# The first attention's values in DRAM: one block per attention unit in place of one row per token

## The chip, the cores and the metric

The kernel runs on one core of a Trainium2 chip. The metric is the device time of one execution in microseconds (us); of several runs the median counts. The core has a matrix engine (TensorE, in the profile PE, its weight loads PEld), a vector engine (DVE), a scalar engine (ACT), a general engine (POOL) and a queue for transfers (SyncE, SP). Transfers between on-chip memory (SBUF) and DRAM run on 16 DMA engines, which all queues share.

## What is computed

Two transformer layers over 1024 latent tokens and 256 context tokens, 1280 in all, 1024 wide. Only the first layer's attention matters here:

```python
p_x, p_c = u_x @ ev_w_in[j], u_c @ ev_w_in[j]
aq, ak, av, bq, bk, bv = split_cols(p, EVEN_SPLITS)      # 6 x 512 columns
# A: 4 differential heads, values 128 wide
a = softmax(q1 k1) - lam * softmax(q2 k2);  o = a @ av
# B: 8 neighbourhood heads, values 64 wide: a query at (row, col) of the 16 x 64 grid reads
# a window of 8 rows x 16 columns of latent keys and all 256 context keys
p = softmax(concat([q k_win * scale + bias, q k_ctx * scale]));  o = p_win @ v_win + p_ctx @ v_ctx
```

## The kernel before, in words

The first layer's projections and its attention are two stages that pass queries, keys and values through DRAM.

**Projection** (`qkv_body`). First come 16 query and key blocks, each of which is stored as 128 rows of 1280 tokens (`sq`, `sk`). Then a loop over z = 0 to 3 and over ten token tiles t computes the values, 256 columns at a time. With z below 2 these are the values of A: the 128 x 256 product is copied out of PSUM into a tile `vf` (tag `qf`, two buffers, ACT and DVE in turn, L481) and stored into `sv` (L482). With z of 2 or 3 they are the values of B, split into a high and a low part: a tile `vs` of 128 x 512 (tags `qh` and `whl` in turn, two buffers each), which is stored into `svb` (L487). The last seven of these stores go out on POOL's queue, all others on SP's.

**Attention** (`attn0`). There are eight units. Units 0 to 3 are the heads of A: a unit loads its queries and keys (12 transfers) and its values, 128 columns of `sv` (`vd`, L1131). Units 4 to 7 are pairs of heads of B: a unit's 256 columns of `svb` are loaded once for the context (`vc`, L1012) and, for each of four column windows j, as four blocks of 4 grid rows x 32 columns (`vs`, L1018), 16 such loads a unit. Each unit of B also needs six bias tables (`tab`, two transfers each, from `rexp`), to which POOL adds a mask (L1030) before DVE uses them.

**What sets the order.** On PE, DVE, ACT and POOL a table of step offsets (`PATTERN`) orders the steps of the jobs; the program's own order rules the transfers of SP. SP takes one transfer after the other: while one waits (for a buffer, for an earlier transfer, for the data to be stored), all behind it wait. A unit's queries and keys are issued during the unit before; `na_hooks` puts the value and table loads of B at fixed jobs. So SP's order at the turn of two units of B is: 12 query and key loads, four `vs`, a store of an output (`so`), four `vs`, two `tab`, `vc`, four `tab`, four `vs`, and so on. POOL also runs in order: a mask whose table has not landed holds up the two memsets (L952, L953) that the next job's transposes on PE need.

Of the kernel before, what the change touches and what calls it, by code (L numbers as in the profile page):

```python
# [10 lines left out]
F32 = mybir.dt.float32  # L11
F32R = mybir.dt.float32r
# [7 lines left out]
P = 128  # L20
# [4 lines left out]
T = NX + NC_  # L25
# [3 lines left out]
HD = 64  # L29
# [51 lines left out]
class Kernel:  # L81
# [211 lines left out]
    def qkv_body(self, es):  # L293
        nc, io = self.nc, self.io
        sb, ps = self.pool(es, "qkv"), self.pool(es, "qkvp", bufs=8, space=PSUM)
        u = [(self.t(sb, [P, KT, 640], f"uh{g}", F32R), self.t(sb, [P, KT, 640], f"ul{g}", F32R)) for g in range(2)]
        w_in = io["ev_w_in"][0].rearrange("(k p) n -> p k n", p=P)
        self.sq = [self.t(self.dram, [2, P, T], f"sq{i}", F32R) for i in range(NU)]
        self.sk = [self.t(self.dram, [2, P, T], f"sk{i}", F32R) for i in range(NU)]
        self.sv = self.t(self.dram, [T, 512], "sv")  # L300
        self.svb = self.t(self.dram, [T, 8, 2, HD], "svb", F32R)
        bg = [(0, ch, hf, 2) for ch in (2, 3, 4, 5) for hf in range(2)]
        bg += [(1, ch, hf, 2) for ch in (0, 1) for hf in range(2)]
        vw = {}
# [6 lines left out]
        def load_w(n):  # L311
            if n < len(cols):
                wf[n] = self.t(sb, [P, KT, P], "wf", bufs=3)
                self.dma(wf[n], w_in[:, :, cols[n]:cols[n] + P])

        def split_v(n):
            z, q = (n - NQ) // 2, (n - NQ) % 2
            if q == 0:
                vw[z] = self.t(vpool, [P, 2, KT, 256], "vw", F32R, bufs=2)
            sl = slice(q * P, q * P + P)  # L320
            self.split(vw[z][:, 0, :, sl], vw[z][:, 1, :, sl], wf[n])

        with ExitStack() as e2:
# [56 lines left out]
            with ExitStack() as e3:  # L380
                st = self.pool(e3, "start")
                h, pt, m = {}, {}, self.modcol[0]
# [59 lines left out]
            def gen_steps(k):  # L442
                accs.extend(a for a in (next(gen) for _ in range(k)) if a)

            def fin():
                for _ in range(len(accs)):
                    self.mod_fin(ps, accs.pop(0))
# [17 lines left out]
            for z in range(4):  # L465
                for t in range(NT):
                    if t in (1, 3):
                        load_w(NQ + 2 * z + (t + 1) // 2 + 2)
                    if t == 0:
                        gen_steps(5)  # L470
                    if t == 8:
                        fin()
                    if t in (4, 6) and z < 3:
                        split_v(NQ + 2 * z + t // 2)
                    g, c0 = t // 5, (t % 5) * P
                    pp = self.t(ps, [P, 256], "ps")
                    self.mm3(pp, lambda k: (u[g][0][:, k, c0:c0 + P], u[g][1][:, k, c0:c0 + P]),
                             lambda k: (vw[z][:, 0, k, :], vw[z][:, 1, k, :]), KT)
                    if z < 2:
                        vf = self.t(qk, [P, 256], "qf", bufs=2)  # L480
                        (nc.scalar.copy if t % 2 else nc.vector.tensor_copy)(vf, pp)  # L481
                        self.dma(self.sv[t * P:(t + 1) * P, z * 256:(z + 1) * 256], vf)  # L482
                    else:
                        vs = self.t(qk, [P, 4, 2, HD], ("qh", "whl")[t % 2], F32R, bufs=2)
                        self.split(vs[:, :, 0, :], vs[:, :, 1, :], pp.rearrange("p (h d) -> p h d", d=HD))

                        (nc.gpsimd if z == 3 and t > 2 else nc.sync).dma_start(  # L487
                            out=self.svb[t * P:(t + 1) * P, (z - 2) * 4:(z - 1) * 4].bitcast(F32), in_=vs.bitcast(F32))


    def rsqrt_exp(self, sb, v, shape, eps):
# [514 lines left out]

    def na_values(self, sb, u, j):

        src = self.svb[:, (u - 4) * 2:(u - 3) * 2].rearrange("t h a d -> t (h a d)")
        if j < 0:  # L1010
            v = self.vs[u, "c"] = self.t(sb, [P, 2, 2, P], "vc", F32R, bufs=2)
            self.dma(v.rearrange("p t h d -> p t (h d)"), src[NX:T, :].rearrange("(t p) c -> p t c", p=P))  # L1012
        else:
            c0 = (0, 8, 24, 32)[j]
            v = self.vs[u, j] = self.t(sb, [P, 4, 2, P], "vs", F32R, bufs=7)
            for rb in range(4):
                sr = src[rb * 256 + c0:rb * 256 + c0 + 1, :]
                self.dma(v[:, rb].rearrange("p h d -> p (h d)"),  # L1018
                         bass.AP(sr.tensor, sr.offset, [[64 * 1024, 4], [1024, 32], [1, 256]]))

    def na_table(self, sb, u, hh, v):

# [95 lines left out]
    def attn_unit(self, sb, ps, u):  # L1118


        qs, ks, ql = (self.t(sb, [P, 2, T], f"{tag}{u % 2}", F32R) for tag in ("qs", "ks", "ql"))
        for m in range(2):
            rows = slice(m * HD, (m + 1) * HD)
            for half in range(2):
                dst = slice(half * HD, (half + 1) * HD)
                self.dma(ks[dst, m, :], self.sk[u][half, rows, :])
                self.dma(qs[dst, m, :], self.sq[u][0, rows, :])
                self.dma(ql[dst, m, :], self.sq[u][1, rows, :])
        if u < 4:
            v = self.t(sb, [P, NT, P], "vd", bufs=2)  # L1130
            self.dma(v, self.sv[:, u * P:(u + 1) * P].rearrange("(t p) c -> p t c", p=P))  # L1131
        unit = (qs, ks, ql)
        if u < 4:
            return self.diff_jobs(sb, ps, u, unit, v)
        return self.na_jobs(sb, ps, u, unit)
# [1640 lines left out]
```

## Time and profile before

| | us |
|---|---|
| median of 3 runs | 3331.13 (3330.67 to 3339.73) |
| the profiled execution | 3333.32 |
| its span, first to last instruction | 3331.5 |
| TensorE busy | 3054.3 (92% of the span) |
| VectorE busy | 2433.3 (73%) |
| DMA, all queues | 444.68 MB in 369192 packets, 133 GB/s over the span |

The span is cut by time into stages: projection of queries and keys to about 330 us, values of A and B to 425 us, the turn to the attention to 450 us, units 0 to 3 to about 680 us, units 4 to 7 to about 890 us. All that the change touches lies in these 560 us; behind them are the output projection, the feed-forward layers and the second layer. A transfer moves its data in packets, here one for each contiguous piece; a packet of under 512 bytes in these views is the end mark of a transfer. "Share of 16 engines" is the packets' time summed over the engines and divided by 16 times the stretch; it can pass 100% where packets on one engine overlap.

### The profile page before, as it was taken

The page shows a single profiled execution, that of the slowest core. Times are in us where ns is not written, and L with a number is a line of the kernel's source. Part 1 is how long each engine was busy: PE and PEld are TensorE (multiplying, and loading weights), DVE is VectorE, ACT ScalarE, POOL GpSimd, SP SyncE. Part 2 cuts the span into 40 slices and gives each one's busy share as a digit, 9 for nine tenths or more (in the row PEclk, how much of TensorE's full clock was granted, in tenths as well). Part 3 has the DMA queues.
Part 4 walks back from the last instruction along what each step waited for, and adds up shares of the span by engine and source line. Part 5 has one row for each costly group of instructions (what it writes and reads, how often), then busy time and mean ns, then how long its engine had stood idle before and what let it go on. Part 6 is the DMA issues. An engine that isn't in the chain of part 4 may idle for free. (4 is left out here: it accounts for less than half of the span.)

```text
span 3331.5 us, 47831 instructions
## 1 busy us (share of the span) xinstructions
PE 3054.3 (92%) x17519; PEld 2711.9 (81%) x17519; DVE 2433.3 (73%) x4109; ACT 1547.1 (46%) x3186; POOL 1003.3 (30%) x780
## 2 busy tenths in 40 slices
PE   7999989975888899889999999989999799999997
PEld 5999878874777899679999788769997688888875
DVE  5776668875788998588997654448887866665576
ACT  5344357774634444333544336237774432333443
POOL 1345445663453221131331002134543301111021
PEclk9999989997998999999999999989999899999998
DMA  7565564375524333644343444274314322225542
GB/s 228 157 216 190 174 173 104 96 172 153 168 76 139 108 112 98 177 144 124 107 145 89 146 151 170 93 230 103 95 39 146 110 74 83 85 80 179 182 135 89
DMA packets 369192, 444.68 MB, mean 133 GB/s; under 512 B 52430, under 2 KB 265071, under 8 KB 365499
## 3 DMA queue, kind: packets, MB, share of 16 engines
q1 hardware_dynamic: 367629, 438.44, 43.5%
q8 instruction: 138, 2.26, 0.3%
q0 software_dynamic: 848, 3.02, 0.3%
q14 instruction: 97, 0.79, 0.1%
q10 hardware_dynamic: 480, 0.16, 0.0%
HBM read 344.51 MB, written 98.18 MB: 133 GB/s over the span
## 5 line engine op out<-in xcount | busy, mean ns | idle before, releaser
L125 PE MATMUL pc<-u,blk 128*128 128x320 f32 (+1 forms) x3540 | 633.0, 336 | 24.7 <-DVE st L1809 7.0
L125 PEld LDWEIGHTS pc<-u,blk 128*128 128x128 f32 x3540 | 573.0, 192 | 66.0 <-DVE blk L1711 7.8
L125 PE MATMUL pa<-blk,blk 128*128 128x512 f32 x1188 | 292.5, 397 | 19.8 <-DVE blk L1711 17.3
L1708 ACT CAST blk<-big 128x512 fp32r<-128x512 f32 x292 | 178.2, 621 | 263.6 <-DVE big L1804 105.0
L1711 DVE TENSOR_TENSOR blk<-wf,blk 128x512 fp32r<-128x512 f32 x377 | 289.2, 769 | 4.5 <-ACT blk L1708 4.5
L125 PEld LDWEIGHTS pa<-blk,blk 128*128 128x128 f32 x1188 | 226.3, 192 | 74.3 <-issue 10.4
L1708 ACT CAST blk<-wf 128x512 fp32r<-128x512 f32 x377 | 232.3, 619 | 111.6 <-PE pc L125 59.6
L1711 DVE TENSOR_TENSOR blk<-big,blk 128x512 fp32r<-128x512 f32 x292 | 212.0, 726 | 57.5 <-ACT blk L1708 57.4
L125 PE MATMUL pa<-u,blk 128*128 128x320 f32 (+1 forms) x1356 | 241.5, 328 | 9.2 <-DVE pt L1809 8.3
L125 PE MATMUL ps<-uh,whl 128*128 128x320 f32 (+2 forms) x1024 | 234.2, 316 | 8.2 <-DVE whl L122 4.8
L125 PEld LDWEIGHTS pa<-u,blk 128*128 128x128 f32 x1356 | 215.5, 190 | 20.6 <-DVE pt L1809 9.0
L125 PE MATMUL pc<-blk,blk 128*128 128x512 f32 x924 | 220.5, 394 | 5.4 <-DVE blk L1711 5.4
L125 PE MATMUL pa<-big,ohl 128*128 128x512 f32 x756 | 201.8, 404 | 19.0 <-POOL ohl L122 4.9
L125 PEld LDWEIGHTS pc<-blk,blk 128*128 128x128 f32 x924 | 175.1, 190 | 42.8 <-ACT u L113 5.8
L247 POOL TENSOR_TENSOR macc<-mw,macc 128x512 f32<-128x512 f32 x96 | 149.3, 1557 | 172.9 <-ACT mw L244 92.6
L820 POOL TENSOR_SCALAR p<-p,rec 128x384 f32<-128x384 f32 (+1 forms) x160 | 143.0, 909 | 177.0 <-DVE rec L635 153.1
L125 PEld LDWEIGHTS pa<-big,ohl 128*128 128x128 f32 x756 | 146.0, 195 | 52.9 <-POOL ohl L122 9.7
L125 PEld LDWEIGHTS ps<-uh,whl 128*128 128x128 f32 x1024 | 176.8, 193 | 11.6 <-DVE whl L122 6.4
L603 ACT ACTIVATE p<-xps,nm 128x1024 f32<-128x1024 f32 x128 | 143.3, 1119 | 80.8 <-DVE nm L599 74.0
L1286 POOL TENSOR_TENSOR r<-r,rowg 128x1024 f32<-128x1024 f32 x32 | 84.0, 2624 | 315.7 <-ACT r L1277 147.2
L624 DVE TENSOR_REDUCE mx<-xps 128x1 f32<-128x1024 f32 x128 | 156.0, 1219 | 18.7 <-PE xps L125 17.8
L125 PE MATMUL ps<-ul,whl 128*128 128x320 f32 (+2 forms) x512 | 161.4, 315 | 1.8 <-DVE ul L415 1.7
(411 smaller groups left out, 6943.9 us busy)
## 6 DMA issues: line engine op xcount, KB each, us to landing
wf<-in_ffn_w_in SPq DMA_DIRECT2D x132, 512.0 KB
wf<-in_ffn_w_out SPq DMA_DIRECT2D x88, 512.0 KB
mw<-in_mod_w SPq DMA_DIRECT2D x64, 512.0 KB
wf<-in_mod_w SPq DMA_DIRECT2D x32, 512.0 KB
uhl<-sun SPq DMA_DIRECT2D x13, 1024.0 KB
wf<-in_ev_w_in SPq DMA_DIRECT2D x24, 512.0 KB
hid<-r SPq DMA_DIRECT2D x22, 512.0 KB
ks<-sk SPq DMA_DIRECT2D x32, 320.0 KB
```

The costliest lines, as they stand in the source:

```text
L125: self.nc.tensor.matmul(out, lhsT, rhs, start=start, stop=stop)
L247: nc.gpsimd.tensor_tensor(out=acc[n][:, conds - 1, :], in0=w, in1=acc[n][:, conds - 1, :], op=ALU.add)
L603: self.nc.scalar.activation(out=out, in_=in_, func=AF.Exp, scale=scale, bias=st["nm"][:, s:s + 1], accum_out=st["sums"][:, s, part:part + 1])
L624: nc.vector.tensor_reduce(out=st["mx"][:, s, 0:1], in_=st["x", s], axis=AX.X, op=ALU.max)
L820: self.nc.gpsimd.tensor_scalar(out=ap, in0=ap, scalar1=rec, scalar2=0.0, op0=ALU.mult, op1=ALU.add)
L1286: self.nc.gpsimd.tensor_tensor(out=e["r"], in0=e["r"], in1=e["rows"]["g"], op=ALU.mult)
L1708: nc.scalar.copy(hi, src)
L1711: nc.vector.tensor_tensor(out=lo, in0=src, in1=hi, op=ALU.subtract)
```

## The change

The two scratch tensors in DRAM get another layout. `sv` was [1280 tokens, 512 columns], so that a token's row held all four units; it becomes [4 units, 1280 tokens, 128 columns]. `svb` was [1280 tokens, 8 heads, 2 parts, 64], and becomes [4 units, 1280 tokens, 256 columns]. A store writes the columns of two units: before one contiguous piece a token (1 KB in `sv`, 2 KB in `svb`), now two pieces of half the size, in two blocks. A load reads the columns of one unit: pieces of the same size as before (512 bytes from `sv`, 1 KB from `svb`), which now lie next to each other in DRAM where they lay 2 KB and 4 KB apart. 112 transfers have another pattern: 20 stores into `sv`, 20 into `svb`, 4 loads of `vd`, 4 of `vc` and 64 of `vs`. On every engine and queue the instructions stand in the same order as before, and each waits for the same things.

```diff
-        self.sv = self.t(self.dram, [T, 512], "sv")
-        self.svb = self.t(self.dram, [T, 8, 2, HD], "svb", F32R)
+        self.sv = self.t(self.dram, [4, T, P], "sv")
+        self.svb = self.t(self.dram, [4, T, 4 * HD], "svb", F32R)
...
-                        self.dma(self.sv[t * P:(t + 1) * P, z * 256:(z + 1) * 256], vf)
+                        self.dma(self.sv[2 * z:2 * z + 2, t * P:(t + 1) * P, :].rearrange("u t c -> t u c"),
+                                 vf.rearrange("p (u c) -> p u c", u=2))
...
-                            out=self.svb[t * P:(t + 1) * P, (z - 2) * 4:(z - 1) * 4].bitcast(F32), in_=vs.bitcast(F32))
+                            out=self.svb[2 * z - 4:2 * z - 2, t * P:(t + 1) * P, :].rearrange("u t c -> t u c").bitcast(F32),
+                            in_=vs.rearrange("p (u h) a d -> p u (h a d)", u=2).bitcast(F32))
...
-        src = self.svb[:, (u - 4) * 2:(u - 3) * 2].rearrange("t h a d -> t (h a d)")
+        src = self.svb[u - 4]
...
-                         bass.AP(sr.tensor, sr.offset, [[64 * 1024, 4], [1024, 32], [1, 256]]))
+                         bass.AP(sr.tensor, sr.offset, [[64 * 256, 4], [256, 32], [1, 256]]))
...
-            self.dma(v, self.sv[:, u * P:(u + 1) * P].rearrange("(t p) c -> p t c", p=P))
+            self.dma(v, self.sv[u].rearrange("(t p) c -> p t c", p=P))
```

## Rows read from the trace of the kernel before

**Rows 1.** Stretches by stage: busy us of each engine, granted clock, DMA share, GB/s.

```profile
core 0: us, PE busy (x) PEld busy (x) DVE busy (x) ACT busy (x) POOL busy (x), PEclk, DMA share, GB/s
330.00:363.00 33.00, 28.11 (x210) 23.32 (x209) 20.50 (x21) 10.89 (x19) 17.92 (x14) 0.95 0.53 154
395.00:425.00 30.00, 29.84 (x255) 29.64 (x255) 21.41 (x25) 12.18 (x22) 18.54 (x13) 1.00 0.54 177
425.00:450.00 25.00, 18.38 (x132) 17.81 (x131) 4.82 (x11) 2.24 (x6) 5.33 (x8) 0.83 1.04 304
450.00:680.00 230.00, 212.16 (x1503) 190.37 (x1502) 202.34 (x403) 172.62 (x437) 128.02 (x65) 0.97 0.49 114
680.00:890.00 210.00, 145.06 (x1074) 136.87 (x1072) 142.52 (x384) 138.53 (x370) 109.73 (x189) 0.87 0.57 158
```

**Rows 2.** Waits, 325 to 442 us: who waited for whom, us, times, longest.

```profile
ACT qf L481 <- DMA sv<-qf: 29.4, 8, 8.3
...
DVE qf L481 <- DMA sv<-qf: 14.2, 3, 7.0
...
PE ps L125 <- DVE qf L481: 4.7, 2, 4.0
```

**Rows 3.** Transfers of 346.3 to 346.85 us: one store into `sv`, alone.

```profile
DMA packets 145, 0.13 MB, mean 242 GB/s; under 512 B 16, under 2 KB 144, under 8 KB 145
...
q1 hardware_dynamic: 145, 0.13, 72.3%
```

**Rows 4.** Transfers of 66 to 67 us: loads in pieces of 512 bytes.

```profile
DMA packets 674, 0.35 MB, mean 354 GB/s; under 512 B 3, under 2 KB 671, under 8 KB 674
...
q1 hardware_dynamic: 674, 0.35, 117.9%
```

**Rows 5.** Transfers of 1999.9 to 2000.4 us: one store in 512-byte pieces.

```profile
DMA packets 48, 0.02 MB, mean 33 GB/s; under 512 B 16, under 2 KB 48, under 8 KB 48
...
q10 hardware_dynamic: 48, 0.02, 15.5%
```

**Rows 6.** Issues on SP and POOL of the tile `sv`, ns min/median/max.

```profile
L109 SPq DMA_DIRECT2D sv<-qf x20: 319/326/882, 330.9 to 380.4; - x20
L109 SPq DMA_DIRECT2D vd<-sv x4: 366/374/377, 440.2 to 568.7; - x4
```

**Rows 7.** Waits, 426 to 470 us.

```profile
POOL p L732 <- ACT p L603: 16.1, 1, 16.1
...
PE b L125 <- DMA ql<-sq: 6.6, 1, 6.6
```

**Rows 8.** Transfers of 408 to 410 us: stores into `svb`, then a weight load.

```profile
DMA packets 379, 0.71 MB, mean 355 GB/s; under 512 B 32, under 2 KB 32, under 8 KB 379
...
q1 hardware_dynamic: 379, 0.71, 95.7%
```

**Rows 9.** Transfers of 397.5 to 398.4 us: one store into `svb`.

```profile
DMA packets 80, 0.16 MB, mean 182 GB/s; under 512 B 0, under 2 KB 0, under 8 KB 80
...
q1 hardware_dynamic: 80, 0.16, 68.2%
```

**Rows 10.** Waits, 680 to 890 us.

```profile
PE xps L830 <- POOL p L953: 45.0, 3, 20.0
POOL tab L1030 <- DMA tab<-rexp: 42.3, 3, 21.7
...
POOL tab L1030 <- DMA vs<-svb: 8.7, 1, 8.7
```

**Rows 11.** SP's instructions in order of time, 743 to 768 us: start us, us.

```profile
743.76 5.76 SPq L109 DMA_DIRECT2D vs<-svb  x4
749.62 3.93 SPq L1002 DMA_DIRECT2D so<-o  x1
753.59 5.14 SPq L109 DMA_DIRECT2D vs<-svb  x4
758.83 2.66 SPq L109 DMA_DIRECT2D tab<-rexp  x2
761.65 0.47 SPq L109 DMA_DIRECT2D vc<-svb  x1
762.22 4.28 SPq L109 DMA_DIRECT2D tab<-rexp  x4
```

**Rows 12.** Transfers of 638 to 639.5 us: loads of `vs` alone.

```profile
DMA packets 143, 0.14 MB, mean 94 GB/s; under 512 B 5, under 2 KB 143, under 8 KB 143
...
q1 hardware_dynamic: 143, 0.14, 27.1%
```

**Rows 13.** Transfers of 46 to 48 us: loads of `h`, rows of 4 KB side by side.

```profile
DMA packets 205, 0.76 MB, mean 379 GB/s; under 512 B 20, under 2 KB 20, under 8 KB 205
...
q1 hardware_dynamic: 205, 0.76, 95.4%
```

**Rows 14.** Issues of the tile `vs` on SP, ns min/median/max.

```profile
L109 SPq DMA_DIRECT2D vs<-svb x64: 515/1290/3665, 623.8 to 858.0; - x64
```

## The prediction

> **What bounds the kernel now.** I read four views in this order: the stretches by stage, the waits of each stage, SP's instructions at the places where a wait ends on a transfer, and the packets of single transfers. By stage [rows 1], TensorE is nearly full while the values of B are computed (29.84 of 30 us) and works 212.16 of 230 us in units 0 to 3, so transfers can hardly cost anything there. It has gaps in three stretches: 33 - 28.11 = 4.9 us in the values of A, 25 - 18.38 = 6.6 us at the turn to the attention, and 210 - 145.06 = 65 us in units 4 to 7. In each gap the wait that ends last ends on a transfer that the change touches, or on one queued behind such a transfer.
>
> In the values of A, ACT waits 29.4 us in 8 places and DVE 14.2 us in 3 until an earlier store into `sv` has given its tile back; TensorE itself waits 4.7 us for it [rows 2]. At the turn, TensorE waits 6.6 us for the first unit's queries [rows 7], while the DMA engines are full (share 1.04). In units 4 to 7 POOL waits 42.3 us for tables, and 8.7 us in a wait that ends with a load of `vs`; TensorE waits 45.0 us in 3 places for the memsets that POOL does behind them [rows 10]. SP shows why the tables are late: from 743.76 us it issues eight `vs` (5.76 + 5.14 us) with a store between them, and only then the tables [rows 11]. So eight `vs` loads stand on the path at each of three turns.
>
> **The change part by part.** No instruction moves and no wait is added or removed. What can change is what a transfer costs its queue, and how long its packets take.
>
> Stores into `sv`. One store alone took 72.3% of 16 engines for 0.55 us, which is 6.36 us of one engine [rows 3], and 6.36 / 128 = 49.7 ns for a piece of 1 KB. The change makes 256 pieces of 512 bytes out of 128 of 1 KB. No store into `sv` of that kind is in the trace; the nearest rows are loads in 512-byte pieces, 1.179 x 16 us / 674 = 28.0 ns each [rows 4], and a small store, 0.155 x 16 x 0.5 / 48 = 26 ns over all its packets, or 1.24 / 32 = 39 ns if its 16 end marks cost nothing [rows 5]. With 28 ns a store takes 256 x 28 - 128 x 49.7 = 0.81 us more engine time, 0.05 us over 16 engines; with 39 ns, 0.23 us. Below, a piece cannot cost less than half of 49.7 ns unless the price per piece vanishes, so the other end is 0. All 11 waits of ACT and DVE end on such a store: 11 x 0.05 = **0.6 us** (0 to 2.5). I take 28 ns because those pieces ran on full engines. The issue grows too: 0.326 us for one piece a partition, 0.374 for ten [rows 6], at most 0.05 us each, and only the three stores just before the first unit's loads have SP's path behind them: 0.1 us.
>
> By the Trainium skill, "DMA: Bandwidth & Descriptors", section "Why small descriptors are slow (HBM only)", a packet costs about three bus cycles beside its 32-byte beats; an estimate from that page is 38 cycles for two pieces of 512 bytes against 35 for one of 1 KB, 9% more, where the rows above say 13%. The trace is thus on the same side as the rule, and the first term would be 0.4 us instead of 0.6 by the rule.
>
> Stores into `svb`. A 2 KB piece took 0.957 x 16 x 2 / (379 - 32) = 88 ns on full engines [rows 8] and 0.682 x 16 x 0.9 / 80 = 123 ns in a stretch with pauses [rows 9]. Two pieces of 1 KB are 2 x 49.7 = 99 ns: 11 ns more or 24 ns less. An engine takes 8 rows of a store, so one store costs +0.09 or -0.19 us. During z = 2 and 3 TensorE is full and hides it. The last ten stores, three on SP and seven on POOL, run while the first unit's loads fill the DMA engines, and there they add to what TensorE waits for: 10 x 0.09 = **0.9 us** (-1.9 to 0.9). I take the dear end because the engines are full there too. POOL itself has room: after its stores it stands idle for 16.1 us [rows 7].
>
> Loads of `vd` and `vc`. Same pieces, same count; `vd` is needed many us after its issue, in units where TensorE is 92% busy. 0.
>
> Loads of `vs`. Here the layout could pay: 32 pieces of 1 KB lay 4 KB apart and now form one run of 32 KB. While only `vs` was moving, 27.1% of 16 engines were busy, 4.3 engines, at 94 GB/s [rows 12]: each load runs on as many engines as it has blocks of rows, four, and those four were full. A piece took 0.271 x 16 x 1.5 / 143 = 45.5 ns, no more than the 49.7 ns of the 1 KB stores [rows 3], which shows no penalty for the gaps that a dense layout could remove. Rows of 4 KB that do lie side by side took 0.954 x 16 x 2 / 185 = 165 ns, 41.2 ns a KB [rows 13]. So the best that contiguity can give is 45.5 - 41.2 = 4.3 ns a piece, 32 pieces an engine, 8 loads and three turns: 4.3 x 32 x 8 x 3 = 3.3 us; if instead a piece cost the dearest 1 KB price of the trace, 49.7 ns, it would be 3.2 us more. I take **0**: the count of pieces, their size and the four blocks are the same. The cost of issuing, 0.515 us at the least and 1.29 us in the middle [rows 14], is set by the four full engines and stays.
>
> Sum: 0.6 + 0.1 + 0.9 + 0 = +1.6 us. On the profiled execution's own 3333.32 us that is 3334.9; this execution lies 2.2 us above the median of the runs shown, so the median comes to 3331.1 + 1.6 = **3332.7 us**. The unknown terms give -5.2 (0 - 1.9 - 3.3) to +6.7 us (2.5 + 0.1 + 0.9 + 3.2), that is 3326 to 3338.
>
> **The rivals.** *The four engines become sixteen.* If the queue saw the run of 32 KB as one thing and spread a `vs` load over all engines, its issue would fall from about 1.3 us to the 0.515 us that it takes when nothing stands in the way [rows 14]. Eight loads at three turns: 0.78 x 8 x 3 = 18.7 us less, 3313 us. For it: those loads stand on the path at every turn [rows 10, 11], and behind them TensorE is plainly idle. Against it: the pattern still begins with four blocks, which are not next to each other, and [rows 12] fit a rule that counts blocks. The Trainium skill, same page, section "Why a DMA increments its semaphore by 16 and not by 1", says just that: the number of engines is the largest up to 16 that divides the slowest dimension of both sides. By that rule it stays at four; the 4.3 engines of the trace agree. 5%.
>
> *Stores pay by the piece.* If a piece of half the size cost what the whole one did, a store into `sv` would take 6.36 / 16 = 0.40 us longer, and one into `svb` 8 x 88 = 0.70 to 8 x 123 = 0.98 us longer. The place is the values of A with their two tiles (11 x 0.40 = 4.4 us) and the turn to the attention (10 x 0.84 = 8.4 us, the middle): 12.8 us, 3344 us, slower. It decides by itself once a half piece costs over about nine tenths of a whole one, where the sum passes 10 us. For it: these stretches do wait on stores and on full engines [rows 1, 2, 7]. Against it: packets grow with their bytes everywhere in the trace, 28 ns at 512 bytes, 49.7 at 1 KB, 88 at 2 KB, 165 at 4 KB [rows 3, 4, 8, 13]. 5%.
>
> *POOL's stores fall behind.* Seven stores go out on POOL's queue beside the first unit's loads. If twice as many pieces a row slow that queue, the loads get past it, and at most TensorE's wait of 6.6 us shrinks [rows 7]; half of it is 3.3 us, 3328 us. Nothing waits for these stores before units 6 and 7, some 300 us on. 8%.
>
> **How the numbers follow.** The forecast, a change of a few us either way from the terms above, has 82%. About 0.3% (10 us) is what a measurement of this kernel can tell from no change; the forecast and the rival on POOL's queue lie within it, save for a few per cent that the stalls in units 4 to 7 react more than term by term, since the granted clock averaged 0.87 of full speed there [rows 1] and a gap that grows or shrinks takes slow time with it. So the same 88%, faster 7%, slower 5%. The range is the bounds of the terms, 3326 to 3338, and 2 us on either side for the spread of the runs, which went up to 3339.73: 3324 to 3340.
>
> **What would show it.** Right: some 4,000 to 5,000 more packets, the stretch with `vs` alone still at about 4.3 engines and 94 GB/s, eight `vs` still 11 us at each turn, POOL's waits for tables within 3 us of 42.3, and a store into `sv` alone at 7 us of engine time. Wrong: `vs` issues near 0.5 us each with a DMA share near 1, or a store into `sv` at 12 us of engine time and TensorE's gap before 340 us wider by some 4 us.

## The result: 0.6% slower, lost in one place at the turn to the attention

The changed kernel takes 3355.52 us (median of 4 runs, 3353.57 to 3357.48) against 3334.68 us (4 runs) for the kernel before: a ratio of 1.0062, 95% interval 1.0047 to 1.0077. The forecast was 3332.7 us, with a range of 3324 to 3340; the measured time lies 15.5 us above its end. The profiled execution spans 3351.8 us where that of before spanned 3331.5 us. Line numbers are one to three higher in the changed kernel (L481 is now L482, L487 is L489, L603 is L606, L732 is L735, L953 is L956).

The stretches by stage of the changed kernel, with the columns of [rows 1], show where the time stands:

```profile
core 0: us, PE busy (x) PEld busy (x) DVE busy (x) ACT busy (x) POOL busy (x), PEclk, DMA share, GB/s
395.00:425.00 30.00, 30.00 (x258) 30.00 (x258) 20.90 (x23) 11.43 (x22) 17.98 (x12) 1.00 0.56 171
425.00:450.00 25.00, 19.03 (x135) 18.02 (x133) 2.27 (x7) 1.86 (x5) 3.60 (x4) 0.81 1.05 266
450.00:490.00 40.00, 17.41 (x83) 13.70 (x82) 18.68 (x34) 14.39 (x35) 8.98 (x7) 0.65 0.63 157
490.00:690.00 200.00, 186.76 (x1357) 168.53 (x1355) 178.13 (x349) 149.80 (x378) 115.76 (x50) 0.99 0.39 94
690.00:910.00 220.00, 154.66 (x1140) 145.60 (x1138) 150.97 (x409) 147.72 (x397) 116.46 (x201) 0.87 0.60 161
```

Up to 425 us nothing is late: the first load of the attention's keys goes out at 425.28 us, before the change at 425.26. From 450 to 490 us TensorE works 17.41 us and its granted clock falls to 0.65; in the same 40 us of the kernel before it worked 35.61 us at 0.89:

```profile
450.00:490.00 40.00, 35.61 (x217) 30.70 (x216) 34.20 (x66) 29.57 (x74) 15.90 (x6) 0.89 0.60 133
```

After that the work runs as before, only later: the first `vs` load goes out at 644.0 us, before at 623.8 [rows 14], and the last at 877.7 instead of 858.0. So about 20 us are lost in one place and carried to the end.

The waits of the changed kernel from 425 to 480 us (who waited for whom, us in total, times, longest) show the chain:

```profile
POOL svb L489 <- issue: 35.2, 5, 9.0
...
PE xps L125 <- ACT p L606: 21.7, 2, 16.1
...
ACT p L606 <- DMA svb<-qh: 17.5, 1, 17.5
ACT whl L113 <- DMA svb<-whl: 14.2, 3, 9.2
...
ACT qh L113 <- DMA svb<-qh: 11.9, 3, 9.4
```

It is read from the end. TensorE waits 21.7 us for ACT's `p`, the exponentials of the first unit. ACT waits 17.5 us before one `p` until a store of `svb` from a tile `qh` has landed: `p` of the attention stands where the projection's tiles stood. Those stores are the last seven, on POOL's queue, and POOL stands 35.2 us at five of them in idle time called "issue", that is, with no other engine and no landing named as the cause. In order of time, POOL's instructions there (start us, us, idle before):

```profile
426.10 1.02 POOL L489 DMA_DIRECT2D svb<-whl  x1
432.96 0.75 POOL L489 DMA_DIRECT2D svb<-qh  x1 [5.83 <-issue]
442.69 0.73 POOL L489 DMA_DIRECT2D svb<-whl  x1 [8.98 <-issue]
452.26 0.73 POOL L489 DMA_DIRECT2D svb<-qh  x1 [8.84 <-issue]
462.87 0.73 POOL L489 DMA_DIRECT2D svb<-whl  x1 [9.88 <-DVE rho L724]
472.58 0.73 POOL L489 DMA_DIRECT2D svb<-qh  x1 [8.98 <-issue]
475.88 0.73 POOL L489 DMA_DIRECT2D svb<-whl  x1 [2.57 <-issue]
```

From the second to the sixth, a store goes out every 9.6 to 10.6 us, and a store took 9.3 us in the middle from issue to landing. One pause, that before 462.87, is put down to a step of DVE (`rho`), but it is as long as the others. When the stores landed can be seen from ACT, which waits for landings to write into the same tiles:

```profile
442.48 0.37 ACT L113 CAST qh<-ps 128x256 fp32r<-128x256 f32 x1 [9.37 <-DMA svb<-qh]
452.05 0.37 ACT L113 CAST whl<-ps 128x256 fp32r<-128x256 f32 x1 [9.20 <-DMA svb<-whl]
...
475.68 1.11 ACT L606 ACTIVATE p<-xps,nm 128x1024 f32<-128x1024 f32 x1 [17.52 <-DMA svb<-qh]
```

In each of these places POOL's next store follows 0.2 us later, at 442.69, 452.26 and 475.88 us: it goes out when the one before it has landed. In the kernel before, the same seven looked like this:

```profile
426.21 0.87 POOL L487 DMA_DIRECT2D svb<-whl  x1
427.14 0.55 POOL L487 DMA_DIRECT2D svb<-qh  x1
427.83 0.54 POOL L487 DMA_DIRECT2D svb<-whl  x1
433.03 0.55 POOL L487 DMA_DIRECT2D svb<-qh  x1 [4.66 <-issue]
...
441.71 0.54 POOL L487 DMA_DIRECT2D svb<-whl  x1 [2.54 <-DVE whl L122]
```

Three went out without a stop. The fourth left at 433.03 us, 0.2 us after ACT's cast at 432.82, which had waited for the landing of the first. The last of the seven left at 441.71 us, now at 475.88. ACT's `p` then starts at 475.68 us, and TensorE's next matmul at 476.94, after its 16.1 us.

**The theory** (called the ring theory in the expectations): POOL writes an entry for every piece of its transfers into a part of SBUF, the ring, whose size the kernel sets, by `dynamic_dma_scratch_size=512` (bytes a partition) in the function `kernel`. An entry's place is free again when the transfer has landed. With 128 pieces a store three stores fit in at a time, with 256 pieces only one, and POOL stands at the next issue until there is room. Its rivals: that twice as many pieces cost the DMA engines that time, or that the layout of `sv`, or both layouts together, does.

### The profile page after: what moved, and what is told of

It reads as the page before. It is cut to its first block, busy times and chain, and to the rows that moved or that the text cites. A ratio compares the mean times of both kernels' runs of the same rounds, so it can differ in the third digit from the quotient of the medians.

```text
span 3351.8 us, 47831 instructions
## 1 busy us (share of the span) xinstructions
PE 3057.2 (91%) x17519; PEld 2715.5 (81%) x17519; DVE 2434.0 (73%) x4109; ACT 1547.9 (46%) x3186; POOL 1001.8 (30%) x780
## 2 busy tenths in 40 slices
DMA packets 373416, 444.68 MB, mean 133 GB/s; under 512 B 52430, under 2 KB 270959, under 8 KB 369723
## 4 chain that ended last, share of the span: by engine, by line
PE 42%; DVE 9%; DMA 3%; issue 2%; ACT 1%; SPq 1%; POOL 1%; ACTq 0%; DVEq 0%; POOLq 0%
PE pc L125 18%; PE pa L125 17%; PE xps L125 2%; DVE blk L1714 2%; PE ops L125 2%; PE b L833 2%; DVE rs_y L1166 1%; DVE big L1807 1%; PE b L125 1%; SPq L109 1%; DVE r L1262 1%; DVE big L2219 1%; DVE r L1256 0%; DMA eh<-hm 0%; ACT eu L1324 0%
## 5 line engine op out<-in xcount | busy, mean ns | idle before, releaser
L606 ACT ACTIVATE p<-xps,nm 128x1024 f32<-128x1024 f32 x128 | 143.4, 1120 | 92.1 <-DVE nm L602 68.7
```

Source lines behind the costliest of these rows:

```text
L606: self.nc.scalar.activation(out=out, in_=in_, func=AF.Exp, scale=scale, bias=st["nm"][:, s:s + 1], accum_out=st["sums"][:, s, part:part + 1])
```

## The experiments

All ratios are to runs of the kernel before on the same chip; the times in one column come from several chips. The table gives, for each kernel, the store sizes on POOL's queue, what the trace shows of POOL, of TensorE's longest wait from 425 to 485 us, and when the first `vs` went out.

| kernel | ring, bytes | pieces a store | issues before the first stop | POOL's idle time at "issue", us | TensorE's longest wait | first `vs`, us | time, us | ratio (95%) |
|---|---|---|---|---|---|---|---|---|
| before | 512 | 128 | 3 | 4.7 | 6.6, `ql` | 623.8 | 3334.68 | 1 |
| after | 512 | 256 | 1 | 35.2 | 16.1, `p` | 644.0 | 3355.52 | 1.0062 (1.0047 to 1.0077) |
| e3 before | 256 | 128 | 1 | 35.8 | 16.4, `p` | 640.0 | 3352.31 | 1.0057 (1.0044 to 1.0070) |
| e5 `svb` only | 512 | 256 | 1 | 35.2 | 16.0, `p` | 639.1 | 3354.25 | 1.0056 (1.0042 to 1.0069) |
| e4 `sv` only | 512 | 128 | 3 | 4.8 | 3.7 | 622.4 | 3334.61 | 1.0004 (0.9995 to 1.0013) |
| e6 after, halves | 512 | 2 x 128 | 3 halves | 24.2 | 6.5, `ql` | 623.8 | 3336.99 | 1.0009 (0.9999 to 1.0018) |
| e2 after | 768 | 256 | 2 | 14.8 | 6.6, `ql` | 622.1 | 3334.54 | 1.0001 (0.9992 to 1.0010) |
| e1 after | 832 | 256 | 3 | 6.9 | 4.3 | 622.0 | 3339.11 | 1.0021 (1.0011 to 1.0031) |
| e10 before | 768 | 128 | 4 or more | 0 | 5.5, `ql` | 620.7 | 3334.61 | 1.0004 (0.9995 to 1.0013) |
| e9 before | 832 | 128 | 4 or more | 0.2 | 3.9 | 619.9 | 3341.14 | 1.0024 (1.0014 to 1.0034) |
| e11 before, other end moved | 768 | 128 | 4 or more | 0.2 | 5.9, `ql` | 621.5 | 3339.38 | 1.0017 (1.0008 to 1.0026) |
| e12 before, `big` and its end moved | 768 | 128 | 4 or more | 0 | 6.5, `ql` | 620.8 | 3340.18 | 1.0019 (1.0010 to 1.0029) |
| e7 after, ACT's queue | - | 256 | - | - | 10.8, `ql` | 628.9 | 3338.99 | 1.0010 (1.0000 to 1.0019) |
| e8 before, ACT's queue | - | 128 | - | - | 13.3, `ql` | 632.2 | 3342.20 | 1.0018 (1.0010 to 1.0027) |

### The ring alone, made larger under the change and smaller under the kernel before

```
-    nc = bacc.Bacc("TRN2", ..., dynamic_dma_scratch_size=512)
+    nc = bacc.Bacc("TRN2", ..., dynamic_dma_scratch_size=768)   # e1: 832; e3, on the kernel before: 256
```

> The changed kernel with 768 bytes for POOL's ring: room for 576 pieces at the least and under 768 by what the two traces show. R expects two stores in flight and never three: pairs of issues some 8 us apart, the seventh at about 450 to 460 us, and 3337 to 3345 us, no faster than the run with 832 bytes. P and S expect 3355 us as with 512 bytes.

> The changed kernel with 832 instead of 512 bytes a partition for POOL's ring of transfer descriptors; nothing else differs. Theory R (the ring is full): before, three stores of 128 pieces were issued back to back (426.21, 427.14, 427.83 us) and the fourth only at 433.03, after the first had landed; after the change each store of 256 pieces waits for the one before (426.10, 432.96, 442.69, ...). So 512 bytes hold three stores of 128 pieces but not two of 256. With 832 bytes there is room for 1.6 times as much, 624 pieces at the least: two stores of 256, perhaps three. R expects the seven stores issued by about 445 to 455 us instead of 476, and 3335 to 3340 us. Theory P (a piece costs POOL's queue more time, whatever the room): the stores keep their pace of about 9.6 us each, 3355 us. Theory S (the layout of DRAM or the stores into sv cost the time): 3355 us.

> The kernel before, old layout, with the ring cut from 512 to 256 bytes: room for one store of 128 pieces, not for two. R expects the old layout to become slow in the same way: each of POOL's stores waits for the one before, the seventh is issued near 470 us, ACT and TensorE wait for it at the start of the first unit, and the time is 3350 to 3357 us. P and S expect no change, 3335 us, since neither the pieces nor the layout differ from before.

POOL's stores with 768 bytes under the change:

```profile
425.54 1.02 POOL L489 DMA_DIRECT2D svb<-whl  x1
426.61 0.74 POOL L489 DMA_DIRECT2D svb<-qh  x1
432.27 0.73 POOL L489 DMA_DIRECT2D svb<-whl  x1 [4.92 <-issue]
435.65 0.72 POOL L489 DMA_DIRECT2D svb<-qh  x1 [2.64 <-issue]
441.53 0.72 POOL L489 DMA_DIRECT2D svb<-whl  x1 [5.15 <-issue]
```

Two are in flight, and the whole loss is gone (1.0001) with the same layouts, pieces and bytes. That is better than expected: 3334.54 us lies below 3337 to 3345. With 256 bytes the kernel before, with none of the change in it, loses what the change lost, and its trace has the same signature, one store at a time:

```profile
423.81 0.87 POOL L487 DMA_DIRECT2D svb<-whl  x1
430.82 0.56 POOL L487 DMA_DIRECT2D svb<-qh  x1 [6.14 <-issue]
440.15 0.54 POOL L487 DMA_DIRECT2D svb<-whl  x1 [8.77 <-issue]
449.38 0.54 POOL L487 DMA_DIRECT2D svb<-qh  x1 [8.69 <-issue]
```

and, among its waits from 425 to 485 us:

```profile
PE xps L125 <- ACT p L603: 23.1, 3, 16.4
...
ACT p L603 <- DMA svb<-qh: 17.4, 1, 17.4
```

So the ring is shown both ways, the loss taken away and made. The theory that the pieces themselves cost the time falls: e2 moves all of them. With the stop gone, nothing of the change is left that can be measured (0.9992 to 1.0010). With 832 bytes three stores of 256 pieces are in flight and the turn is no later than before (first `vs` at 622.0 us), yet the time is 4.6 us above that with 768. That was not expected; e9 and e10 below look into it.

### Each half of the change alone

e4 takes only the new layout of `sv`, e5 only that of `svb`, each with the stores and loads that belong to it (left out here):

```
-        self.sv = self.t(self.dram, [T, 512], "sv")
+        self.sv = self.t(self.dram, [4, T, P], "sv")
...
-        self.svb = self.t(self.dram, [T, 8, 2, HD], "svb", F32R)
+        self.svb = self.t(self.dram, [4, T, 4 * HD], "svb", F32R)
```

> Only the first half of the change: sv lies unit by unit, svb as before. R expects 3335 us, within 1.5 us of the kernel before on the same chip (by the prediction's first term 0.6 us, and 0.1 us for issuing). P expects the same. S expects the 20 us here, 3355 us.

> Only the second half of the change: svb lies unit by unit (its stores have 256 pieces), sv as before; the ring of POOL's queue at its 512 bytes. Ring theory: the seven stores of svb on POOL's queue go one at a time, as in the changed kernel (4 issues stopped by <-issue for about 9 us each), TensorE waits about 16 us for ACT's p near 475 us, and the time is 3350 to 3357 us, the whole loss of the change. If the loss came from sv or from the two layouts together, it would be near 3335 us.

The half on `sv` costs nothing that can be measured (3334.61 us, 1.9 us above the kernel before on that chip, where 1.5 was expected; the interval of its ratio reaches 0.9995), the half on `svb` the whole loss. `svb` is the tile whose last seven stores are on POOL's queue; `sv` is stored on SP's alone.

### The same pieces in twice as many stores

```
-                        (nc.gpsimd if z == 3 and t > 2 else nc.sync).dma_start(
...
+                        vu = vs.rearrange("p (u h) a d -> p u (h a d)", u=2)
+                        if z == 3 and t > 2:
+                            for i in range(2):
+                                nc.gpsimd.dma_start(out=self.svb[2 + i, rows, :].bitcast(F32), in_=vu[:, i].bitcast(F32))
...
```

> The changed kernel, but each of the seven svb stores on POOL's queue is issued as two stores, one for each unit, of 128 pieces of 1 KB. The bytes, the pieces and the places in DRAM are the same. Ring theory: the ring, which held three stores of 128 pieces in the kernel before and one of 256 in the changed one, holds three halves, that is one and a half stores, so the next store starts before the last has landed: an issue is stopped less long than the 9 us, TensorE's wait for ACT's p near 475 us falls from 16.1 us to between 5 and 12 us, and the time lies between those of the ring with one store and with two, 3336 to 3346 us. If the cost hung on the bytes or pieces that the queue moves, it would stay at 3350 to 3357 us.

The issues in order of time show the halves: the stops are shorter (24.2 us in 8, the longest 6.0), ACT's wait before `p` is 5.1 us, TensorE's 4.3 us, a little less than expected, and the time is 3336.99 us. With 512 bytes and 256 pieces a tile, what matters is whether the next transfer has to wait for the whole of the last one.

### Another queue

```
-    (nc.gpsimd if z == 3 and t > 2 else nc.sync).dma_start(
+    (nc.scalar if z == 3 and t > 2 else nc.sync).dma_start(
```

> The changed kernel with the seven svb stores issued on ACT's queue in place of POOL's. Ring theory: no issue stands at POOL's ring, so TensorE's 16.1 us wait for ACT's p near 475 us goes; ACT waits at each issue for DVE's half of the tile, about 0.5 to 1 us, seven times, on an engine that waits 3 to 5 us for TensorE at each of these evictions anyway. 3328 to 3338 us. It falls if the time stays above 3345 us.

> The kernel before with its seven svb stores on ACT's queue in place of POOL's. In the kernel before, three stores in flight leave ACT waiting 16.1 us for landings in the stretch, but TensorE's longest wait there is 6.6 us for the load of ql, not for a store. Ring theory: little to win, 3326 to 3335 us; a gain over 0.3% would mean that the ring held back the kernel before as well.

On ACT's queue no issue is stopped and ACT has no 17.5 us wait; the ring's loss is gone in e7, whose 3338.99 us lies 1 us above what was expected. But neither kernel is better than the kernel before, and e8, where little change was expected, is slower (1.0018). (In the expectation of e8 the 16.1 us are POOL's wait of [rows 7]; ACT's waits for these landings were 8.3 and 7.2 us.) In both, TensorE's wait for the first unit's `ql` grew, from 6.6 us [rows 7] to 10.8 and 13.3 us. I had put such a wait down to the DMA engines being crowded. The trace of e8 says otherwise: from 425 to 450 us they moved 206 GB/s at a share of 0.77, where before they were full [rows 1]. SP's waits of e8 in that stretch:

```profile
SPq L109 <- DMA svb<-qh: 10.5, 3, 5.1
SPq L109 <- DMA svb<-whl: 7.3, 3, 3.8
```

SP, which issues `ks`, `qs` and `ql`, waits 17.8 us for the landing of the stores that ACT has issued. In the kernel before no wait of SP there ends on a store of `svb`. In the program as built, each of those loads waits on a semaphore that a store of ACT has raised: the two hardware queues are given their semaphores from one set, in turn, and a load that gets the semaphore of a store in flight stands until that store has landed. POOL's stores have semaphores of their own. This is read from the trace and the program; no run gave the loads other semaphores. So the place on POOL's queue is worth something, and its ring is the price.

### The ring's size with the old stores

> The kernel before with 832 bytes for POOL's ring in place of 512. With 512 it held three stores of 128 pieces; by the ratio 832/512 it should now hold four or five, so POOL's issues are stopped less (three stops of 4.66, 3.39 and 2.54 us before) and the stores crowd the load of ql more, for which TensorE waited 6.6 us before and 13.3 us where the stores went on ACT's queue without a stop. Crowding theory: that wait is between 6.6 and 13.3 us and the time 3334 to 3342 us, the same as with a ring of 768 bytes. Size theory (the changed kernel with 832 bytes came out 5 us above that with 768 by something that has nothing to do with the stores, such as where the tiles then lie): about 5 us above the kernel with 768 bytes, at the same wait for ql.

> The kernel before with 768 bytes for POOL's ring in place of 512: by the ratio it holds four or five stores of 128 pieces in place of three. Crowding theory: TensorE waits 6.6 to 13.3 us for ql, and the time is 3334 to 3342 us, the same as with 832 bytes. Size theory: about 5 us below the kernel with 832 bytes, at the same wait for ql. If neither the ring nor the crowding matters beyond three stores, it stays at 3331 to 3336 us.

The diff is that of the first experiment, on the kernel before. (Of the three stops that the expectation of e9 names, only the first, of 4.66 us, is a stop at issue; the other two end on DVE's part of the tile that is to be stored.) Crowding falls here too: with four or more stores in flight TensorE's longest wait is shorter (5.5 us for `ql`, and 3.9 us with no releaser), not longer. And 832 bytes is slower than 768 by 6.5 us without the change, by 4.6 us with it, though the turn is earlier in both (first `vs` at 619.9 and 622.0 us). The cost lies elsewhere. The matmuls of TensorE grouped by operands over the whole span (count, busy us, mean ns, idle time before), for e2 and then e1:

```profile
L125 PE MATMUL pc<-big,blk 128*128 128x512 f32 x468 | 111.3, 389 | 0.0
L125 PE MATMUL pa<-big,blk 128*128 128x512 f32 x216 | 51.9, 389 | 0.0
```

```profile
L125 PE MATMUL pc<-big,blk 128*128 128x512 f32 x468 | 114.3, 394 | 0.0
L125 PE MATMUL pa<-big,blk 128*128 128x512 f32 x216 | 53.3, 394 | 0.0
```

The rows of e10 and e9 for these two groups read the same, 389 and 394 ns. With `pa<-big,ohl` (200.3 to 206.6 us, and 202.1 to 205.0) these matmuls take 10.7 us longer in e1 than in e2 and 7.3 us longer in e9 than in e10, more than twice the 4.6 us and a little more than the 6.5 us of the times.

### The tiles' places without the ring

The ring lies first in SBUF, so its size moves all tiles behind it; `big` and about twenty other tiles (`r`, `q`, `k`, `v`, `w` among them) are laid out from the other end and stay. Two kernels keep the ring at 768 bytes and move tiles by 64 bytes with an unused tile: e11 those of the first end, as 832 bytes had done, and e12 those of the other end, `big` with all the others there (not `big` alone, as its expectation has it):

```
         c = self.cst
+        self.pad = self.t(c, [P, 16], "pad")                             # e11
...
+        self.pad = self.t(self.rpool(es, "padr"), [P, 16], "pad")       # e12
         self.r0 = self.rpool(es, "big")
```

> The kernel before with a ring of 768 bytes and an unused tile of 64 bytes a partition ahead of the others, so that all tiles but big, which is laid out from the other end of SBUF, stand where they stood with a ring of 832. Place theory: the matmuls on big take 394 ns in the mean as with 832 bytes, not 389, and the time is 3338 to 3343 us, above that of the kernel with 768 bytes (3334.61). If the cost of 832 bytes comes from the ring itself, the matmuls stay at 389 ns and the time at 3332 to 3337 us.

> The kernel before with a ring of 768 bytes and an unused tile of 64 bytes a partition at the other end of SBUF, so that big alone moves by 64 bytes and blk, the tile that it is multiplied with, stays. If it is the distance between big and blk that counts, the matmuls on big take 394 ns and the time is 3338 to 3343 us, as with 832 bytes. If it is the place of blk alone, they stay at 389 ns and the time at 3332 to 3337 us.

e11 took 3339.38 us (1.0017, 1.0008 to 1.0026) and e12 3340.18 us (1.0019, 1.0010 to 1.0029). The same matmuls, for e11 and then e12:

```profile
L125 PE MATMUL pc<-big,blk 128*128 128x512 f32 x468 | 114.3, 394 | 0.0
```

```profile
L125 PE MATMUL pc<-big,blk 128*128 128x512 f32 x468 | 114.3, 394 | 0.0
```

Both are slow, and the ring is the same as in e10. So it is neither the ring nor the place of `blk` alone. It fits that what counts is where the two operands lie to each other: matmuls on two tiles `blk`, which moved together in e11, stayed as they were (924 of them at 392 ns in e10 and 393 in e11). That `big` and `blk` moved together would be fast was not tried, so a rule for the place of each by itself is not shut out. Both kernels bring the two tiles 64 bytes nearer to each other, at 5 ns a matmul; the 256 bytes between the rings of 512 and 768 cost nothing (389 ns in both). Other distances were not tried, and why they count stays open. This accounts for e1: its stores and the turn were as the ring theory wanted, and its 4.6 us above e2 come from tiles that the ring had pushed aside.

None of the kernels beats the kernel before.

## Why the prediction was wrong

**What bounds the kernel.** The stages and waits were read rightly as far as they went. The turn to the attention was named as a place where time could be lost, but only for TensorE's wait on `ql`.

**Stores into `sv`: right.** The waits for them, with the columns of [rows 2], are now

```profile
ACT qf L482 <- DMA sv<-qf: 25.3, 7, 9.7
...
DVE qf L482 <- DMA sv<-qf: 15.7, 3, 8.4
```

41.0 us in 10 places where there were 43.6 in 11; the term was +0.6 us, and e4 measures nothing. A piece costs what the loads of [rows 4] gave. From 344.4 to 345 us the changed kernel has

```profile
DMA packets 311, 0.15 MB, mean 252 GB/s; under 512 B 16, under 2 KB 311, under 8 KB 311
...
q1 hardware_dynamic: 311, 0.15, 91.9%
```

which is 0.919 x 16 x 0.6 us / 311 = 28.4 ns a packet. The issue on SP grew from 0.326 to 0.367 us in the middle, the 0.05 us that was allowed.

**Stores into `svb`: the step that failed.** The term of 0.9 us counted engine time of their pieces alone. The step behind it was "POOL itself has room: after its stores it stands idle for 16.1 us". That idle time lies after the stores; what ran out lies during them, and the two lines of [rows 7] do not show it. The trace of before did, and the view of [rows 7] has it further down, as `POOL svb L487 <- issue: 4.7, 1, 4.7`: the fourth store of POOL stood 4.66 us for no engine and no landing that is named, right after three had gone out. That is a bound reached at three transfers of 128 pieces, and the change doubles the pieces. So "no wait is added" holds for the waits that the program names, not for POOL's issues: they stood 35.2 us at "issue" and the kernel lost 20.8 us, where the prediction had put the whole term at 0.9 us.

The engine time itself, which the term counted, did not grow on POOL's queue. From 425 to 480 us this queue (q0) moved, before and then after:

```profile
q0 software_dynamic: 560, 1.84, 10.2%
```

```profile
q0 software_dynamic: 560, 1.84, 10.3%
```

Of the 560 packets 7 x 16 are end marks (e6, with seven stores more, has 672), and the other 448 hold 4 KB each: two of the old pieces, four of the new. So "one for each contiguous piece" is not so on this queue. The packets took 89.8 us of one engine before and 90.6 after, which is 0.05 us more over 16 engines where the seven stores were to cost 7 x 0.09 = 0.6. Bytes, packets and engine time stayed; the pieces for which POOL needs room in the ring doubled.

By the Trainium skill, "DMA: Bandwidth & Descriptors", sections "Terms" and "The descriptor swizzle", a transfer of POOL is written as 16-byte descriptors into rings in SBUF, and one to 128 partitions has, on each engine, 8 for data and one for its end, on the reading and on the writing side alike. An estimate from that page, if the bytes of one partition are one engine's ring, is 32 descriptors in 512 bytes: three stores of 9 (27) before, one of 17 (two would be 34) after; 768 bytes hold two of 17 (34 of 48), 832 three (51 of 52), 256 one of 9. The runs agree at each of these sizes, with 3, 1, 2, 3 and 1 issues before the first stop; no view shows the descriptors themselves.

**Loads of `vd`, `vc` and `vs`: right.** While only `vs` moves, from 657.5 to 659 us of the changed kernel, the transfers answer to [rows 12]:

```profile
DMA packets 140, 0.14 MB, mean 94 GB/s; under 512 B 4, under 2 KB 140, under 8 KB 140
...
q1 hardware_dynamic: 140, 0.14, 27.1%
```

The same share and rate: a load still runs on four engines, though its 32 pieces now lie next to each other. Its issue is 514/1301/3598 ns, in [rows 14] 515/1290/3665. Eight `vs` at the turn take 6.05 + 5.13 us, in [rows 11] 5.76 + 5.14. The waits from 690 to 910 us answer to [rows 10]:

```profile
PE xps L833 <- POOL p L956: 43.6, 3, 20.1
POOL tab L1033 <- DMA tab<-rexp: 40.4, 3, 21.7
```

**The rivals.** *Four engines become sixteen* did not happen (its 3313 us is 3312.4 by its own terms, 3331.1 - 18.7; nothing rests on it). *Stores pay by the piece* had the sign and 12.8 of the 20.8 us (3344), by the wrong mechanism: a piece costs by its bytes, and e2, with all pieces, is level with the kernel before. Its nearness is luck. *POOL's stores fall behind* had the right place and the wrong sign. Its reason was "Nothing waits for these stores before units 6 and 7, some 300 us on". That holds for the data. It does not hold for the tiles the stores read from: ACT's and DVE's next two tiles wait for them, and then `p` of the first unit, which takes their place in SBUF. In the kernel before ACT already waited for these landings, 8.3 us at `qh` and 7.2 us at `whl`, hidden by the work that TensorE still had.

**What would show it.** Nearly every sign that was named for a right forecast came true: 373416 packets, 4,224 more than before, which is 128 for each of the 33 stores on SP; `vs` at 94 GB/s; 11 us for eight `vs`; 40.4 us for the tables. The time was still wrong, since no sign was named for the one queue on which the changed transfers do not go out through SP.

## What to carry to other kernels

Where a change makes the pieces of a transfer smaller, look at which queue issues it: on POOL's queue count the pieces in flight against the ring, and take a stop called "issue" behind the n-th transfer as a sign that n is all it holds. Ask of a later store not only who reads its data but who takes over the tile it reads from, and look for that tile's successor past the end of the stage. And a remedy is a change too: another queue held up loads, a ring of 832 bytes moved tiles to a dearer place, and 768 bytes, or stores cut in halves, only brought the change back to level.

## What the runs showed that was not expected

- POOL stops at issue when its ring is full, and the trace shows it as idle time before the issue: 8.98 us between stores of 256 pieces with 512 bytes, none between the first three of 128.
- Stores issued on ACT's queue held up loads on SP's by 17.8 us in 6 waits, though the DMA engines had room (share 0.77).
- POOL's queue packed the pieces into packets of 4 KB, so that halving the pieces changed neither its packets (560) nor their engine time (10.2 and 10.3% of 16 engines for 55 us).
- A matmul's time depends on where its operands lie in SBUF: with the tiles at one end of SBUF moved by 64 bytes against those at the other, 684 matmuls on the tile `big` went from 389 to 394 ns in the mean, and the whole kernel lost 0.17 to 0.19% (e11, e12).
